# First product of a feed-forward network: seven products of quarters, or the plain product of 512 tokens at once

## The chip, the cores and the metric

The kernel runs on one core of a Trainium2 chip. The metric is the device time of one execution in microseconds; of several runs the median is given. The engines are named as the profile names them: PE (TensorE), PEld (its weight loads), DVE (VectorE), ACT (ScalarE), POOL (GpSimd), SP (SyncE, which issues most of the transfers).

## The reference

Two layers of a transformer work on 512 tokens of 1024 numbers and, in the first layer, on 256 context tokens beside them. A layer has a mixing half (a linear recurrence and differential attention) and a feed-forward half. Only the second concerns us here:

```python
def sq_relu_mlp(h, w1, w2):
    return jnp.square(jax.nn.relu(h @ w1)) @ w2      # w1: 1024 x 4096, w2: 4096 x 1024

f = sq_relu_mlp(modulate(rms_norm(x, g_pre_mlp[l]), sh2, s2), w_ff1[l], w_ff2[l])
x = x + g2 * rms_norm(f, g_post_mlp[l])
```

All is in float32. In layer 0 the context tokens take the same way, so that 768 tokens go through both products; in layer 1 only the 512 do.

## The kernel before

**Exact products.** Each float32 operand is split in a rounded upper part and the rest (`unit` for weights, lines 1496 and 1497: a copy on ScalarE, a subtraction on VectorE; `split_s` for the squares, lines 1653 and 1654). `mm3` (line 351) then adds three products for each pair: upper by upper, upper by rest, rest by upper.

**Blocks.** The 4096 hidden columns are taken in eight blocks `b` of 512. For a block, `ff1(b)` makes the squares `sq` (four tiles of 128 hidden columns by all tokens), and `ff2(b)` multiplies them with the second weights and adds to `acc` and `U2`. Block 0 has a plain first product (`ff1_plain`, in groups of 256 tokens), block 7 a plain second one (`end`, after `put`). So a layer runs `ff1_plain`, `ff2(0)`, `ff1(1)`, `ff2(1)`, up to `ff1(7)`, `end`.

**Seven products.** All other products go by the identities of Strassen and Winograd. Tokens, inner rows and columns are halved (`W` is half the tokens, 384 in layer 0 and 256 in layer 1), and seven products of quarters with sums of quarters replace the eight of the plain way. In `ff1` a product multiplies 512 rows by 256 columns of weights with half of the tokens: 24 matmuls of 128 x 128 weights with `W` columns. The sums cost extra work:

- sums of weights, on GpSimd, in `seven` (lines 1514 to 1518): four subtractions of 128 x 1024 for each block and each product, and seven units to split in place of four;
- sums of tokens, once a layer, between `ff2(0)` and `ff1(1)`: `tokens_sums` and `last_sum` (lines 1571 to 1600), on VectorE, GpSimd and ScalarE;
- sums of products: in `ff1` the `gather` of line 1621 on VectorE and a copy on ScalarE (line 1627), in `ff2` the `gather` of line 1687, and sums of squares on GpSimd (line 1669).

**Weights and places.** The weights come through six places of 1024 columns (`places`); `load` issues the transfer on SP's queue, `unit` splits. Split units lie in places of their own, used in turn (`wus`): three in layer 0, six in layer 1. `stream` hands out the units in the order of use, and `weights()` keeps three of them ahead. The products of `ff1` go to four banks of the accumulator memory (`pm`), those of `ff2` to four others (`pmg`); `bank` takes them in turn.

**Order.** The program is written in the order of the blocks; the framework reorders the instructions of the engines by its own model of time, within what the data allow, so that parts of `ff1(b + 1)` stand between those of `ff2(b)`.

Of the kernel before, what the change touches and what calls it, by code (L numbers as in the profile page):

```python
# [20 lines left out]
T = 768  # L21
TC = 256
EM = math.exp(-0.5)
# portions of projection work per portion of attention, by layer
FILLS = [2.3, 4.5]
# portions of adaLN work per recurrence step, by layer
# [28 lines left out]
def shape_consts():  # L55
# [8 lines left out]
    # the second direction's removal rows and columns lie reversed in each block of 32, so that its blocks, too,  # L64
    # are upper triangular
# [61 lines left out]
def ZI(a, p):  # L127
    """row of zd: a = 0, 1, 2 for r, k and the normalized k, p the pair of heads."""
    return (p // 2) * 6 + a * 2 + p % 2


class Fill:
    """Emits side work in small portions between the portions of the main work."""
# [31 lines left out]
class K:  # L165
# [91 lines left out]
    def ada_half(self, l, ch, hf, ps, tag):  # L257
        """512 adaLN columns for (c, c_ctx): columns 128*g.. as rows 32*g and 32*g+1, without bias."""
        nc = self.nc
        acc = ps.tile([128, 128], F32, name=self.n("adar"), tag=tag, bufs=1 if tag == "a" else 2)  # L260
        for kp in range(4):
            raw = self.raw(self.I["ada_w"][l, ch, hf, kp // 2][:, 2 * (kp % 2):2 * (kp % 2) + 2], [128, 2, 512])
            for k in range(2):
                for g in range(4):
                    nc.tensor.matmul(acc[32 * g:32 * g + 32, :], self.sc[:, 2 * kp + k, :],
                                     raw[:, k, g * 128:g * 128 + 128], start=(kp + k == 0), stop=(kp == 3 and k == 1),
                                     skip_group_check=True)
            if kp < 3:
                yield
        self.acc = acc  # L270
# [53 lines left out]
    def halves(self, src, shape):  # L324
        """loads of the two halves of a piece of weights."""
# [17 lines left out]
    def mm3(self, out, pairs, step=8, start=True):  # L343
        """out = sum over (sh, sl, mh, ml) of stationary^T moving, operands split exactly in two; added to what out
        holds if not `start`."""
# [15 lines left out]
    def new_hT(self):  # L361
        """split activations, one [128, T] view per 128 rows; the upper four lie first."""
# [7 lines left out]
    def norm(self, x, xn, junk):  # L370
        """xn = rms(x), the gain left out."""
# [7 lines left out]
    def norm_T(self, xn, group, mods, hT, pool, ps, toks):  # L379
        """two normed tiles [128,1024] of the tokens from toks on: modulated, transposed, split."""  # L380
# [22 lines left out]
    def layer(self, l):  # L403
        nc, I = self.nc, self.I
        last = l == L - 1
        if l == 0:
# [5 lines left out]
            with ExitStack() as es:  # L412
                # the first weights take the place of x
# [59 lines left out]
    def phase_wr(self, l, last):  # L473
# [33 lines left out]
        # The projections are cut into units: products into one bank, then its evacuation, which is emitted  # L507
        # only when the next unit's products have begun. Small units that follow from one wait in `posts`.
# [202 lines left out]
        def stream(order):  # L711
# [9 lines left out]
            for n, p in enumerate(order):  # L721
                wh, wl = w
                nxt = lambda: self.split_w(None, [128, 8, 256], feed(), wpw[(n + 1) % 2])
                if p >= 11:
                    both = order[n:n + 2] == [11, 12]
                    if both:
                        # the first tiles of both pieces run while the last tiles are still being normed
# [108 lines left out]
        def subln(j):  # L836
            """rms norm per head of a pair of heads, and its transposed store."""
# [88 lines left out]
    def recurrence(self, l, last, es, side):  # L926
        """opens the recurrence; its first sets go to `side`. Returns what emits the rest."""
# [4 lines left out]
        # a pool each: what comes after the recurrence may take a place as soon as it is free  # L932
# [13 lines left out]
        # zeros beside each head's rows and beside each half of the low-rank inputs let products run over 128 rows  # L946
# [15 lines left out]
        def prep_a(n, d, pp):  # L962
            """decay and rate of one pair of head pairs over one tile of 128 tokens, one direction."""
# [25 lines left out]
        def prep_b(n, d, pp, ld, th, ta):  # L989
            """chunk matrices of that pair from decay and rate."""  # L990
            need_y = not (last and n < 2)
            if pp == 0:
                # the same tile for every third group: each part is taken again as soon as it has been read
# [13 lines left out]
            # tokens in blocks of 32; the second direction's reversed in each  # L1007
# [16 lines left out]
            # half of it: the rate and its mix with k come doubled  # L1024
# [16 lines left out]
            # a bank for each head of the pairs: the heads lie in different rows  # L1041
# [37 lines left out]
        def relay(n, d):  # L1079
            # diagonal 32-blocks to one matrix per partition: (the block that the merge takes first, d, p, c, hf)  # L1080
# [12 lines left out]
        def eliminate(N, W, n):  # L1093
            """W, the rows 2i + (partition >= 64) of the strictly upper N, to those of (I - N)^-1."""
# [13 lines left out]
        def inv(n):  # L1108
            """inverses of the diagonal blocks of a group back into G, the transposed ones for the merge beside it."""
# [34 lines left out]
        def merge(n):  # L1144
# [11 lines left out]
            # the rows that each half of the partitions held come one after the other in TT  # L1156
# [87 lines left out]
        def finish(ti):  # L1244
# [8 lines left out]
            else:  # L1253
                # the sets of the groups that are over make room for it
# [49 lines left out]
        def rest():  # L1304
# [20 lines left out]
            for n in range(6):  # L1325
# [5 lines left out]
                for j in range(2):  # L1331
                    nst = 0
                    for _ in step(n, j):
# [5 lines left out]
                        # the next group but one: what it waits for is longer than a step  # L1339
# [19 lines left out]
    def post_norm(self, ob, Gb, x, junk):  # L1359
        """x += rms(ob) * Gb, in place in x."""  # L1360
# [15 lines left out]
    def phase_o(self, l, last):  # L1376
# [6 lines left out]
        with ExitStack() as es:  # L1383
# [18 lines left out]
            # what the first pairs need comes first  # L1402
# [39 lines left out]
    def phase_f(self, l, last):  # L1442
        """Most products go by Strassen's and Winograd's identities: seven products of halves of the tokens, of the rows
        and of the columns of a piece of weights give the eight that the product has. Tokens' sums s1 = a21 + a22,
        s2 = s1 - a11, s3 = a11 - a21, s4 = a12 - s2; weights' sums t1 = b12 - b11, t2 = b22 - t1, t3 = b22 - b12,
        t4 = b21 - t2; with u = a11 b11 + s2 t2 and v = u + s1 t1 the quarters are a11 b11 + a12 b21, u + s1 t1 + s4 b22,
        u + s3 t3 + a22 t4 and v + s3 t3."""
# [8 lines left out]
        # the halves of the tokens  # L1456
# [3 lines left out]
        with ExitStack() as es:  # L1460
            # the squares and their sums lie first: they end early, and the next layer's first weights take their place
# [16 lines left out]
            # six places of 1024 columns  # L1478
# [11 lines left out]
            def unit(src, m, pool=None):  # L1490
                """1024 columns of weights as m rows, split."""
# [8 lines left out]
            def seven(quarter, m, order, start=None):  # L1500
                """The weights of the seven products, in the order given."""
# [17 lines left out]
                # those that end first are taken again first  # L1519
                at = {"t1": 0, "t4": 1, "t3": 2, "b22": 3, "t2": 4}  # L1520
                places[:] = [places[i] for i in [5] + [at[k] for k in order if k in at]]

            def stream():
                for b in range(8):
                    if b:
                        yield from seven(lambda k, c: lines(k, c, b), 4, order1(b))
# [8 lines left out]

            def order1(b):
                return ["b11"] + (["t2", "b21"] if b > 1 else ["b21", "t2"]) + ["t1", "t3", "b22", "t4"]
# [33 lines left out]
            whole = lambda x, a, g, k: nc.vector.tensor_tensor(x, *(hT[f, g][:, k, H[a]].bitcast(F32) for f in "hl"), add)  # L1571

            def keep(x, S, k):
                nc.scalar.activation(S[0][:, k], x, AF.Copy)
                nc.vector.tensor_tensor(S[1][:, k], x, S[0][:, k].bitcast(F32), sub)

            def tokens_sums(S1, S2, pool):
                """The sums of the halves of the tokens, split; s3 takes a21's place."""
                S3 = tuple(hT[f, 0][:, :, H[1]] for f in "hl")
                f = nc.gpsimd.tensor_tensor  # L1580
                for k in range(4):
                    a11, a21, a22 = (pool.tile([128, W], F32, name=self.n("fx"), tag=f"x{i}") for i in range(3))
                    whole(a21, 1, 0, k)
                    whole(a22, 1, 1, k)
                    whole(a11, 0, 0, k)
                    f(a22, a21, a22, add)
                    f(a21, a11, a21, sub)
                    f(a11, a22, a11, sub)
                    keep(a22, S1, k)
                    keep(a11, S2, k)  # L1590
                    keep(a21, S3, k)
                return S3

            def last_sum(S2, S4):
                f = nc.gpsimd.tensor_tensor
                for k in range(4):
                    x = t2.tile([128, W], F32, name=self.n("fx"), tag="x", bufs=3 if last else 1)
                    whole(x, 0, 1, k)
                    for s in S2:
                        f(x, x, s[:, k].bitcast(F32), sub)  # L1600
                    keep(x, S4, k)

            def ff1(b, S):
                S1, S2, S3, S4 = S
                A = {(a, k): tuple(hT[f, k][:, :, H[a]] for f in "hl") for a in range(2) for k in range(2)}
                # u and v are in place in the quarters that come last
# [200 lines left out]
```

## Time and profile before

| | |
|---|---|
| median of 3 runs | 2538.57 us (2533.5 to 2541.35) |
| profiled execution | span 2535.5 us from its first instruction to its last; no time of its own is listed beside it |
| PE, DVE busy | 2264.5 us (89%), 1774.2 us (70%) |
| products of layer 0 from `ff2(0)` to `ff1(7)` | 876.3 to 1348.9 us |
| the same of layer 1 | 2123.2 to 2504.5 us |

The span is about 3 us shorter than the median of the runs. The window of a stage is cut at the first product with `fah` (the split squares) and at the end of `ff1(7)`.

### The profile page before, as it was taken

The page shows a single profiled execution, that of the slowest core. Times are in us where ns is not written, and L with a number is a line of the kernel's source. Part 1 is how long each engine was busy: PE and PEld are TensorE (multiplying, and loading weights), DVE is VectorE, ACT ScalarE, POOL GpSimd, SP SyncE. Part 2 cuts the span into 40 slices and gives each one's busy share as a digit, 9 for nine tenths or more (in the row PEclk, how much of TensorE's full clock was granted, in tenths as well). Part 3 has the DMA queues.
Part 4 walks back from the last instruction along what each step waited for, and adds up shares of the span by engine and source line. Part 5 has one row for each costly group of instructions (what it writes and reads, how often), then busy time and mean ns, then how long its engine had stood idle before and what let it go on. Part 6 is the DMA issues. An engine that isn't in the chain of part 4 may idle for free. (4 is left out here: it accounts for less than half of the span.)

```text
span 2535.5 us, 45036 instructions
## 1 busy us (share of the span) xinstructions
PE 2264.5 (89%) x17486; PEld 1948.9 (77%) x17486; DVE 1774.2 (70%) x2875; ACT 1246.6 (49%) x2551; POOL 1005.5 (40%) x1144
## 2 busy tenths in 40 slices
PE   6999998899889979999989999999799887798787
PEld 5897887777769868888878877788678776687676
DVE  5456459567655697777787465756665648999997
ACT  4345457544444444444435345655454445454543
POOL 1213225823122475555552322324621126665561
PEclk8999998788999999999999999997788798899999
DMA  6544344577685111111114353534676542112222
GB/s 263 150 132 110 124 132 108 129 186 190 170 240 185 51 59 67 67 67 67 67 58 171 108 162 101 156 108 109 165 191 146 151 167 84 67 67 100 91 76 108
DMA packets 291636, 313.75 MB, mean 124 GB/s; under 512 B 139680, under 2 KB 220896, under 8 KB 291424
## 3 DMA queue, kind: packets, MB, share of 16 engines
q1 hardware_dynamic: 280320, 284.66, 36.9%
q0 software_dynamic: 10240, 23.08, 4.8%
q8 instruction: 138, 2.26, 0.4%
q10 hardware_dynamic: 864, 3.15, 0.3%
q14 instruction: 74, 0.61, 0.1%
HBM read 257.04 MB, written 53.77 MB: 123 GB/s over the span
## 5 line engine op out<-in xcount | busy, mean ns | idle before, releaser
L1497 DVE TENSOR_TENSOR wl<-raw,wh 128x1024 fp32r<-128x1024 f32 x212 | 324.6, 1538 | 28.2 <-ACT wh L1496 28.1
L1496 ACT ACTIVATE wh<-raw 128x1024 fp32r<-128x1024 f32 x212 | 219.8, 1054 | 150.4 <-PE pf L351 45.2
L351 PE MATMUL pf<-wh,fah 128*128 128x512 f32 x570 | 238.4, 421 | 60.7 <-ACT fs L1546 18.4
L351 PE MATMUL pf<-wl,fah 128*128 128x512 f32 x570 | 235.5, 414 | 14.9 <-DVE wl L1497 14.8
L351 PE MATMUL pf<-wh,fal 128*128 128x512 f32 x570 | 224.5, 412 | 8.1 <-DVE fal L1654 8.1
L351 PE MATMUL pu<-hh,wh 128*128 128x512 f32 (+1 forms) x632 | 223.6, 354 | 3.4 <-DVE t L557 1.7
L351 PE MATMUL pu<-hh,wl 128*128 128x512 f32 (+1 forms) x632 | 218.1, 346 | 3.8 <-DVE wl L340 3.8
L351 PE MATMUL pu<-hl,wh 128*128 128x512 f32 (+1 forms) x632 | 217.8, 345 | 0.0
L351 PEld LDWEIGHTS pf<-wh,fah 128*128 128x128 f32 x570 | 113.6, 199 | 98.7 <-DVE acc L1687 22.2
L351 PE MATMUL pf<-hh,wh 128*128 128x256 f32 (+1 forms) x608 | 181.2, 307 | 8.6 <-ACT wh L1496 3.4
L351 PE MATMUL pf<-hh,wl 128*128 128x256 f32 (+1 forms) x608 | 180.5, 305 | 3.7 <-DVE wl L1497 3.4
L351 PE MATMUL pf<-hl,wh 128*128 128x256 f32 (+1 forms) x608 | 183.8, 305 | 0.0
L797 DVE TENSOR_REDUCE nm<-sc 128x1 f32<-128x768 f32 (+1 forms) x160 | 132.7, 842 | 70.3 <-PE sc L795 69.3
L799 ACT ACTIVATE e<-sc,nm 128x768 f32<-128x768 f32 (+1 forms) x160 | 131.1, 823 | 50.2 <-DVE nm L797 38.8
L321 POOL TENSOR_TENSOR rs<-ms,pw 128x1 f32<-128x1 f32 (+2 forms) x60 | 56.9, 951 | 233.4 <-DVE ms L319 232.2
L351 PEld LDWEIGHTS pf<-wl,fah 128*128 128x128 f32 x570 | 113.8, 200 | 40.3 <-DVE wl L1497 17.8
L680 POOL TENSOR_TENSOR zs<-zpad 128x512 f32<-128x512 f32 (+1 forms) x51 | 47.8, 937 | 240.2 <-ACT zpad L678 228.9
L351 PEld LDWEIGHTS pf<-wh,fal 128*128 128x128 f32 x570 | 112.5, 198 | 37.9 <-DVE fal L1654 12.3
L351 PEld LDWEIGHTS pu<-hh,wh 128*128 128x128 f32 x632 | 120.7, 191 | 21.5 <-DVE t L557 2.3
L351 PEld LDWEIGHTS pu<-hh,wl 128*128 128x128 f32 x632 | 120.8, 191 | 18.9 <-DVE wl L340 4.7
L832 PEld LDWEIGHTS po<-vn,pT 128*128 128x128 f32 x832 | 115.7, 209 | 23.6 <-ACT pT L818 13.7
L351 PEld LDWEIGHTS pu<-hl,wh 128*128 128x128 f32 x632 | 120.8, 191 | 14.3 <-issue 1.7
(281 smaller groups left out, 6658.4 us busy)
## 6 DMA issues: line engine op xcount, KB each, us to landing
raw<-in_w_ff SPq DMA_DIRECT2D x128, 512.0 KB
raw<-in_ada_w SPq DMA_DIRECT2D x96, 512.0 KB
raw<-in_w_in SPq DMA_DIRECT2D x52, 512.0 KB
ld<-zd SPq DMA_DIRECT2D x40, 384.0 KB
ks<-qd POOLq DMA_DIRECT2D x64, 192.0 KB, 5.7
zd<-zr SPq DMA_DIRECT2D x22, 384.0 KB
raw<-in_w_out SPq DMA_DIRECT2D x16, 512.0 KB
qs<-qd POOLq DMA_DIRECT2D x32, 192.0 KB, 6.0
```

What stands on the lines that cost most here:

```text
L321: nc.gpsimd.tensor_tensor(r, m, self.pw1.to_broadcast([128, cols]), ALU.pow)
L351: nc.tensor.matmul(out, a, b, start=(start and i == 0 and j == 0), stop=(i == n - 1 and j == 2), skip_group_check=not start)
L680: nc.gpsimd.tensor_tensor(s[:, sl], z[:, a - 1:b - 1], z[:, a + 1:b + 1], ALU.add)
L797: nc.vector.tensor_reduce(nm, sc, AX.X, ALU.max, negate=True)
L799: nc.scalar.activation(ee, sc, AF.Exp, bias=nm, accum_out=ls[:, br:br + 1])
L832: nc.tensor.matmul(po, pT[:, k * 128:k * 128 + 128], vn[:, k, h * 64:h * 64 + 64], start=(k == 0), stop=(k == nk - 1))
L1496: nc.scalar.activation(hi, src, AF.Copy)
L1497: nc.vector.tensor_tensor(lo, src, hi.bitcast(F32), sub)
```

## The change

In both layers the first product of blocks 1 to 7 is made plainly. `four` takes the place of `seven` for these weights: it loads and splits the four pieces of 1024 columns as they are. `ff1(b)` takes two units (the two halves of the 1024 rows, for 256 columns), and for each 128 of its columns adds 8 x 3 matmuls with 512 tokens at once, and, in layer 0, 8 x 3 more with the last 256. Each finished bank is squared by ScalarE (`square`: Relu, then Square in place). The sums of tokens and the tiles for them, the order of the seven products, and the sums of line 1621 go away. `ff2` and `end` stay. `ff1_plain` gets its extra place for weights in both layers, where before layer 1 had none.

```diff
+            def four(b):
+
+                ts = [load(2 * c + k, lines(k, c, b)) for c in range(2) for k in range(2)]
+                for t in ts:
+                    yield unit(t, 4)
+                places[:] = places[4:] + places[:4]
 
             def stream():
                 for b in range(8):
                     if b:
-                        yield from seven(lambda k, c: lines(k, c, b), 4, order1(b))
+                        yield from four(b)
                     if b < 7:
                         yield from seven(lambda k, c: cells(k, c, b), 2,
                                          ["b11", "b21", "t3", "t4", "t2", "t1", "b22"], None if b else self.normed)
...
-            def order1(b):
-                return ["b11"] + (["t2", "b21"] if b > 1 else ["b21", "t2"]) + ["t1", "t3", "b22", "t4"]
...
-            def tokens_sums(S1, S2, pool):
...
-            def last_sum(S2, S4):
...
-            def ff1(b, S):
-                S1, S2, S3, S4 = S
...
-                X = times(A[0, 0], weights())
-                for i in range(2):
-                    nc.scalar.copy(U[i], X[i])
-                for k in order1(b)[1:3]:
-                    if k == "t2":
-                        gather(U, times(S2, weights()), U)
-                    else:
-                        times(A[0, 1], weights(), X)
-                        for i in range(2):
-                            square(C11[i], X[i])
-                Y = times(S1, weights())
-                gather(V, Y, U)
-                X = times(S3, weights())
-                gather(V, X, V, True)
-                times(S4, weights(), Y)
-                gather(C12, Y, U, True)
-                times(A[1, 1], weights(), X)
-                gather(U, X, U, True)
+            def ff1(b):
+
+                for c in range(4):
+                    if c % 2 == 0:
+                        w = [weights(), weights()]
+                    cs = slice(c % 2 * 128, c % 2 * 128 + 128)
+                    for t0, t1 in ((i0 * 128, i0 * 128 + 512),) + (() if last else ((512, T),)):
+                        p = bank(t1 - t0)
+                        self.now(self.mm3(p, [(w[k // 4][0][:, k % 4, cs], w[k // 4][1][:, k % 4, cs],
+                                               hh[k][:, t0:t1], hl[k][:, t0:t1]) for k in range(8)]))
+                        square(sq[c][:, t0 - i0 * 128:t1 - i0 * 128], p)
...
             with ExitStack() as es2:
-                s_pool = lambda e: self.pool(e, "fh", 1)
-                s_tiles = lambda p: tuple(p.tile([128, 4, W], F32R, name=self.n("fh" + f), tag="f" + f) for f in "hl")
-                S2, S1 = [s_tiles(s_pool(es2)) for _ in range(2)]
-                # what comes before s4 lies in its place
-                with ExitStack() as es3:
-                    ff1_plain(None if last else self.pool(es3, "wx", 1))
+                ff1_plain(self.pool(es2, "wx", 1))
                 ff2(0)
-                with ExitStack() as e:
-                    for i in behind:
-                        e.enter_context(tc.issue_after(i))
-                    with ExitStack() as es3:
-                        S3 = tokens_sums(S1, S2, self.pool(es3, "fx", 3 if last else 2))
-                    S4 = s_tiles(s_pool(es2))
-                    last_sum(S2, S4)
-                S = S1, S2, S3, S4
                 for b in range(1, 8):
-                    ff1(b, S)
+                    ff1(b)
                     if b < 7:
                         ff2(b)
```

All other lines of the diff drop comments.

## Rows read from the trace of the kernel before

**Rows 1.** The page's table of engines: busy us, share of the span, instructions.

```profile
PE 2264.5 (89%) x17486; PEld 1948.9 (77%) x17486; DVE 1774.2 (70%) x2875; ACT 1246.6 (49%) x2551; POOL 1005.5 (40%) x1144
```

**Rows 2.** Windows: length, PE, PEld, DVE, ACT, POOL busy, granted clock, DMA share, GB/s.

```profile
1184.40:1247.87 63.47, 59.78 (x296) 52.44 (x295) 49.16 (x59) 29.60 (x46) 31.90 (x17) 1.00 0.20 67
2366.65:2417.39 50.74, 42.10 (x254) 36.56 (x253) 49.98 (x53) 25.39 (x47) 29.17 (x17) 0.97 0.26 83
876.30:1348.90 472.60, 431.22 (x2060) 377.27 (x2059) 386.96 (x445) 222.52 (x357) 250.46 (x130) 0.97 0.19 66
2123.20:2504.50 381.30, 314.41 (x1788) 271.95 (x1789) 368.71 (x401) 191.47 (x353) 223.54 (x131) 0.91 0.24 82
```

**Rows 3.** Timeline of ScalarE: the copies that mark a block; start, us.

```profile
1184.40 0.48 ACT L1627 COPY fs<-pf 128x384 f32<-128x384 f32 x1 [6.07 <-PE pf L351]
...
1247.87 0.48 ACT L1627 COPY fs<-pf 128x384 f32<-128x384 f32 x1 [6.08 <-PE pf L351]
...
2366.65 0.35 ACT L1627 COPY fs<-pf 128x256 f32<-128x256 f32 x1
...
2417.39 0.35 ACT L1627 COPY fs<-pf 128x256 f32<-128x256 f32 x1
```

**Rows 4.** Timeline of TensorE: first and last of runs without a gap.

```profile
1130.12 0.34 PE L351 MATMUL pf<-hh,wh 128*128 128x384 f32 x1
...
1150.26 0.34 PE L351 MATMUL pf<-hh,wl 128*128 128x384 f32 x1
...
1154.32 0.39 PE L351 MATMUL pf<-wh,fal 128*128 128x512 f32 x1
...
1173.14 0.40 PE L351 MATMUL pf<-wl,fah 128*128 128x512 f32 x1
...
1179.91 0.40 PE L351 MATMUL pf<-wh,fah 128*128 128x512 f32 x1
...
2235.20 0.28 PE L351 MATMUL pf<-hh,wh 128*128 128x256 f32 x1
...
2239.64 0.28 PE L351 MATMUL pf<-fhl,wh 128*128 128x256 f32 x1
```

**Rows 5.** Timeline of TensorE: two gaps, and a product after one.

```profile
1157.07 0.47 PE L351 MATMUL pf<-wh,fah 128*128 128x512 f32 x1 [2.36 <-DVE fu L1687]
...
1158.26 0.63 PE L351 MATMUL pf<-wl,fah 128*128 128x512 f32 x1
...
2406.72 0.47 PE L351 MATMUL pf<-wh,fah 128*128 128x512 f32 x1 [4.72 <-ACT fs L1546]
```

**Rows 6.** VectorE by line, one block of layer 1 (2366.65 to 2417.39).

```profile
L1497 DVE TENSOR_TENSOR wl<-raw,wh 128x1024 fp32r<-128x1024 f32 x14 | 22.8, 1642 | 0.8 <-ACT wh L1496 0.8
L1654 DVE TENSOR_TENSOR fal<-ts,fah 128x256 fp32r<-128x256 f32 x8 | 10.4, 1342 | 0.0
L1687 DVE TENSOR_TENSOR acc<-pf,acc 128x512 f32<-128x512 f32 x11 | 7.3, 675 | 0.0
...
L1621 DVE TENSOR_TENSOR fs<-pf,fs 128x256 f32<-128x256 f32 x10 | 4.0, 410 | 0.0
```

**Rows 7.** Instructions on the tiles fs and wl: ns min/median/max, first and last start.

```profile
L1621 DVE TENSOR_TENSOR fs<-pf,fs x140: 406/483/560, 942.5 to 2504.8; 128x384 f32<-128x384 f32 x70, 128x256 f32<-128x256 f32 x70
...
L1654 DVE TENSOR_TENSOR fal<-fs,fah x100: 405/620/2754, 869.4 to 2506.6; 128x384 fp32r<-128x384 f32 x50, 128x256 fp32r<-128x256 f32 x50
...
L1497 DVE TENSOR_TENSOR wl<-raw,wh x212: 1205/1224/3434, 799.4 to 2498.2; 128x1024 fp32r<-128x1024 f32 x106
```

**Rows 8.** GpSimd by line, the same block of layer 1.

```profile
L1514 POOL TENSOR_TENSOR raw<-raw,raw 128x1024 f32<-128x1024 f32 x3 | 7.2, 2409 | 5.7 <-DMA raw<-in_w_ff 5.7
```

**Rows 9.** VectorE by line, beginning of the stage in layer 1 (2118 to 2215).

```profile
L1575 DVE TENSOR_TENSOR fhl<-fx,fhh 128x256 fp32r<-128x256 f32 x12 | 15.0, 1276 | 0.5 <-ACT fhh L1574 0.5
L1571 DVE TENSOR_TENSOR fx<-hh,hl 128x256 f32<-128x256 f32 x16 | 11.8, 782 | 0.0
```

**Rows 10.** Timeline of TensorE, last block of layer 0.

```profile
1322.37 0.69 PE L351 MATMUL pf<-fhh,wl 128*128 128x384 f32 x1 [3.21 <-DVE wl L1497]
```

More of the change, by code (lines that the diff above doesn't have):

```diff
@@ L1569, in ff1_plain @@
                 places[:] = [places[i] for i in (1, 2, 3, 4, 5, 0)]
[L1571 to L1575, printed above, removed]
-            def tokens_sums(S1, S2, pool):
[L1579 to L1592, printed above, removed]
@@ L1594, in last_sum @@
-            def last_sum(S2, S4):
[L1595 to L1601, printed above, removed]
-            def ff1(b, S):
-                S1, S2, S3, S4 = S
-                A = {(a, k): tuple(hT[f, k][:, :, H[a]] for f in "hl") for a in range(2) for k in range(2)}
-                C11, C12, U, V = [[sq[2 * c + i][:, HS[a]] for i in range(2)] for a in range(2) for c in range(2)]
-                def times(a, w, old=None):
-                    res = []
-                    for i in range(2):
-                        cs = slice(i * 128, i * 128 + 128)
-                        p = old[i] if old else bank(W)
-                        self.now(self.mm3(p, [(w[0][:, k, cs], w[1][:, k, cs], a[0][:, k], a[1][:, k])
-                                              for k in range(4)], start=old is None))
-                        res.append(p)
-                    return res
-                def gather(d, p, x, done=False):
-                    for i in range(2):
-                        nc.vector.tensor_tensor(d[i], p[i], x[i], add)
-                        if done:
-                            square(d[i])
-                X = times(A[0, 0], weights())
-                for i in range(2):
-                    nc.scalar.copy(U[i], X[i])
-                for k in order1(b)[1:3]:
-                    if k == "t2":
-                        gather(U, times(S2, weights()), U)
-                    else:
-                        times(A[0, 1], weights(), X)
-                        for i in range(2):
-                            square(C11[i], X[i])
-                Y = times(S1, weights())
-                gather(V, Y, U)
-                X = times(S3, weights())
-                gather(V, X, V, True)
-                times(S4, weights(), Y)
-                gather(C12, Y, U, True)
-                times(A[1, 1], weights(), X)
-                gather(U, X, U, True)
```

## The prediction

> **What bounds the kernel now.** I read the engine table first [rows 1]: TensorE is busy 89% of the span, VectorE 70%. These are averages over very different stages, so the next view is busy time by stretch [rows 2], cut where the change acts: the feed-forward stage of each layer, from the first product with the second weights to the start of the last block's plain end. It lasts 472.6 us in layer 0 and 381.3 us in layer 1; each holds seven blocks (`ff2(0)` to `ff1(7)`). To cut one steady block I took the same copy (L1627, the evacuation that begins `ff1`) in two neighbouring blocks [rows 3]: 63.5 us in layer 0, 50.7 us in layer 1. In these windows [rows 2] the two layers differ. In layer 1 VectorE is busy 49.98 of 50.74 us: it is the bound there, and TensorE waits for it. In layer 0 VectorE has 14 us to spare, and TensorE is nearly always at work.
>
> Busy TensorE time contains modelled ends, so I price products from start to start in runs without a gap [rows 4]: 256 columns take (2239.64 - 2235.20) / 37 = 0.120 us, 384 take (1150.26 - 1130.12) / 116 = 0.174 us, and 512 take (1179.91 - 1173.14) / 29 = 0.233 us in a run beside other work. The 17 that follow the last of 384 columns up to 1154.32 need (1154.32 - 1150.26 - 0.174) / 17 = 0.229 us; I use 0.231. All at full clock.
>
> Products of one block, all three exact-split passes counted, before the change. Layer 0: `ff1` 7 x 2 x 4 x 3 = 168 of 384 columns = 29.2 us, `ff2` 7 x 3 x 2 x 3 = 126 of 512 = 29.1 us, sum 58.3. Layer 1: 168 of 256 = 20.2, 84 of 512 = 19.4, sum 39.6. So a steady block holds 5.2 us in layer 0 and 11.1 us in layer 1 that are no product. Where they lie [rows 5]: in layer 0 TensorE waits 2.36 us for VectorE in `ff2`, and then runs at the lower of its two clocks for a while (a product of 0.63 us where others take 0.40 [rows 4]); I put eight such at 8 x 0.23 = 1.8 us. In layer 1 the largest gap is 4.72 us at the start of `ff2`, after the last square of `ff1`.
>
> **What the change does to TensorE.** `ff1` becomes 4 x 8 x 3 = 96 products of 512 columns, and in layer 0 another 96 of 256. Layer 0: 96 x 0.231 + 96 x 0.120 = 33.7 us against 29.2, that is 4.5 more per block; the block's floor goes from 58.3 to 62.8. Layer 1: 22.2 against 20.2, 2.0 more; floor 41.6. Over seven blocks and two layers the plain products add 45 us to TensorE. This loss is certain; the rest must pay for it.
>
> **What it does to VectorE.** Per block it takes away three of fourteen weight splits (`wl`, L1497) and all ten sums of L1621. At today's means in layer 1 [rows 6] this is 3 x 1.64 + 4.0 = 8.9 us of 50.0, leaving 41.1. How far it can fall further is seen from the spread of single instructions [rows 7]: L1621, which reads one operand from PSUM, never exceeds 560 ns, while the splits, which read both from SBUF, go from 405 to 2754 ns (L1654) and from 1205 to 3434 (L1497). I put the long ones down to GpSimd, which reads SBUF at the same time. With no stretch VectorE would need 11 x 1.21 + 14 x 0.405 + 14 x 0.675 = 28.4 us. GpSimd loses half of its weight sums (four of eight of 2.4 us, [rows 8]), some 10 of its 29 us [rows 2], so I expect about 36. Either way VectorE ends below TensorE's 41.6 us, and TensorE becomes the bound in layer 1.
>
> **ScalarE** loses three weight copies per block; the evacuations become four wide Relu and four Square (eight of each in layer 0). It is busy 25 to 30 us per block [rows 2]: no bound. The loads stay four pieces per product, 67 and 83 GB/s in these windows; I cost them at nothing, hidden by the splits and products between. Were that cover gone, `raw` would be late for the copies of L1496, and the price would be a gap of the kind of the next paragraph.
>
> **What remains idle.** Layer 1's 4.72 us should go: today `ff2` waits for quarters finished by the last of the seven products; in the plain order the first product of `ff2` reads squares of the first two column tiles, done half an `ff1` earlier. The gap that stays is that of the bank whose partial sum must be read before more is added to it, with its slow clock. From 11.1 I keep 4.0 per block in layer 1 (bounds 1.5 and 6.0). In layer 0 I keep 3.0 of 5.2 (bounds 1.0 and 5.2), as part of the GpSimd work that delays VectorE there remains. So a block takes 65.8 us in layer 0 (was 63.5) and 45.6 in layer 1 (was 50.7).
>
> **The beginning.** Before `ff1(1)` the sums of halves of the tokens are made (L1571 to L1600). Seven steady blocks would be 7 x 63.5 = 444.4 and 7 x 50.74 = 355.2 us; the stages take 472.6 and 381.3, so their beginnings (and, in layer 0, a late stall) cost 28.2 and 26.1 us. In layer 1 the token sums keep VectorE for 11.8 + 15.0 us [rows 9] and a little more while it is saturated. The change drops them. The first block still has its first weights to split and no lead; I leave 8 us in layer 0 (bounds 4 and 14) and 9 in layer 1 (5 and 14).
>
> **Sum.** Layer 0: 7 x 65.8 + 8 = 468.6 us, 4.0 less than 472.6. Layer 1: 7 x 45.6 + 9 = 328.2, 53.1 less than 381.3. Together 57 us off a span of 2535.5; the median of the runs shown, 2538.57, lies 3.1 above that span, so 2538.6 - 57 = 2481.5, and I say 2481. With all lower bounds: layer 0 7 x 63.8 + 4 = 450.6 (-22), layer 1 7 x 43.1 + 5 = 306.7 (-75): 2442. With all upper: 7 x 68.0 + 14 = 490 (+17), 7 x 47.6 + 14 = 347 (-34): 2522.
>
> **Rivals.** *VectorE stays the bound in layer 1.* If the 12 GpSimd instructions left per block (four of 2.4 us and eight sums of tokens' squares, some 9 us) each hold VectorE for their whole length, it needs 28.4 + 18.7 = 47.1 us, and at today's 98.5% share a block takes 47.8: 7 x 47.8 + 9 = 343.6, the gain shrinks to 4 + 38 = 42 us, 2497. For it: the stretched splits above. Against: at today's means VectorE needs 41 only. The Trainium skill states this as a rule (SBUF — State Buffer, section "Who interferes with whom"): a VectorE instruction with two SBUF inputs and a GpSimd one that reads SBUF exclude each other for a whole instruction, whoever comes second waits. This case's spread agrees (2754 against at most 560 ns); by the strictest reading this rival is the forecast, and I give it 13%.
>
> *Three places for split weights in layer 0.* Plain `ff1` holds two units at once and needs the fourth when the first has just come free, 12 products of 256 columns (1.4 us) before the next pair begins; its copy and split must fit into that and 12 of 512 (2.8 us). With stretched splits they don't: a stall like the 3.21 us on `wl` late in layer 0 [rows 10] and 1.8 us of slow clock in each block, 7 x 5.0 = 35 us; the gain falls to 22 us, 2516. Against: an unstretched copy and split take under 2.5 us. 7%.
>
> *The turn from `ff1` to `ff2` stalls (slower).* The last tile's Relu, Square and split lie in one chain on ScalarE and VectorE; if `ff2` must wait for it as today in layer 1 (4.72 us [rows 5] and 1.8 of slow clock), each of 14 blocks pays 6.5 us, 91 in all, against a gain of 57: 34 slower, 2572. It decides from 57 / 14 = 4.1 us per block on. Against it: one product of `ff2` (12 or 18 matmuls, 2.8 or 4.2 us) needs none of the last tile and covers most of that chain. 6%; that it costs about 4 us a block, and nothing is left, 4%.
>
> *Nearly no idle time remains* (lower bounds): 2442 or a little below, 6%.
>
> **Chances.** Forecast 64%, VectorE 13, weight places 7, turn 6 and 4, lower bounds 6. Measurement tells about 0.3% (7.6 us) from no change. Faster: 64 + 13 + 7 + 6 = 90%; same 4%; slower 6%. The range 2444 to 2520 takes in the forecast's bounds, the VectorE and the weight-place rival, and leaves out the turn and half of the lower bounds.
>
> **What would show it.** Right: no L1571 to L1621 lines; `pf<-hh,wh` of 512 columns started 0.23 us apart; steady blocks of 64 to 68 us in layer 0, longer than before, and 43 to 48 in layer 1, shorter; VectorE under 90% there; splits with a lower mean; `ff2(0)` to `ff1(1)` without saturated VectorE. Wrong: 512-column products further apart than 0.24 us or at the lower clock, TensorE idle before `fah` or before the second pair of weights in each block, a VectorE still at 98% in layer 1, or a beginning as long as before (waiting for first weights or their GpSimd sums, not for the token sums).

## The result and the profile after

| | median, us | range of the runs, us | runs |
|---|---|---|---|
| before, on the same chip | 2539.2 | 2533.5 to 2541.35 | 4 |
| after | 2450.86 | 2442.96 to 2465.64 | 4 |

The ratio is 0.9648, 95% interval 0.9612 to 0.9685: 88 us off, where 57 were forecast. The time lies inside the range (2444 to 2520), near its fast end.

The profiled execution after has a span of 2463.9 us and is the slowest of the four. The page's table of engines, to be held against [rows 1]:

```profile
PE 2273.2 (92%) x17150; PEld 1919.2 (78%) x17150; DVE 1516.6 (62%) x2629; ACT 1173.8 (48%) x2393; POOL 806.8 (33%) x1048
```

TensorE is busy longer than before (2273.2 against 2264.5) in a shorter span. VectorE lost 258 us and GpSimd 199. Busy time by stretch of the kernel after (length, PE, PEld, DVE, ACT, POOL busy, granted clock, DMA share, GB/s). The first two stretches are four blocks of layer 1 and three of layer 0; the other two are the stages of layer 0 and layer 1, cut as in [rows 2]:

```profile
2221.27:2386.64 165.37, 165.37 (x722) 135.15 (x721) 129.40 (x156) 84.98 (x133) 74.39 (x48) 1.00 0.31 102
1066.83:1259.81 192.98, 189.36 (x956) 158.91 (x955) 112.47 (x138) 75.81 (x124) 64.49 (x37) 1.00 0.20 66
879.90:1333.85 453.95, 443.85 (x2229) 371.38 (x2227) 267.67 (x325) 187.62 (x308) 146.25 (x82) 1.00 0.21 68
2129.90:2427.00 297.10, 293.17 (x1261) 238.34 (x1261) 230.28 (x279) 155.92 (x248) 122.77 (x81) 0.99 0.33 108
```

The blocks were cut at the same evacuation in neighbouring blocks, now a Relu; timeline of ScalarE, kernel after (start, length):

```profile
1066.83 0.60 ACT L1549 ACTIVATE fs<-pf 128x512 f32<-128x512 f32 x1 [5.18 <-PE pf L351]
...
1131.08 0.60 ACT L1549 ACTIVATE fs<-pf 128x512 f32<-128x512 f32 x1 [5.23 <-PE pf L351]
...
2221.27 0.58 ACT L1549 ACTIVATE fs<-pf 128x512 f32<-128x512 f32 x1
...
2262.45 0.58 ACT L1549 ACTIVATE fs<-pf 128x512 f32<-128x512 f32 x1
...
2386.64 0.58 ACT L1549 ACTIVATE fs<-pf 128x512 f32<-128x512 f32 x1
```

A block of layer 0 takes 192.98 / 3 = 64.33 us (before 63.47), one of layer 1 165.37 / 4 = 41.34 (before 50.74). In layer 1 TensorE has no idle time left in four blocks; VectorE is busy 129.40 / 4 = 32.4 us of 41.3, where it was 49.98 of 50.74 [rows 2]. GpSimd fell from 29.17 to 18.6 us per block. The bound has moved from VectorE to TensorE, and 180 products of 512 columns in 41.34 us make 0.2297 us each.

The stages, cut from the first product with the second weights to the last of `ff1(7)`'s `pf<-hl,wh`, in the two profiled executions:

| us | before | after | difference |
|---|---|---|---|
| stage of layer 0 | 472.2 | 453.7 | -18.5 |
| between the stages | 774.7 | 796.3 | +21.6 |
| stage of layer 1 | 381.1 | 296.7 | -84.4 |
| end of layer 1's stage to the last instruction | 31.2 | 37.3 | +6.1 |

With 3.6 more ahead of layer 0's stage this is the span's -71.6. The last line of the table is a shift: 24 products of the final block that used to stand between the last ones of `ff1(7)` now come behind them. The 21.6 us between the stages lie in work that the change does not touch, and are taken up at the end.

### The profile page after: what moved, and what is told of

It is laid out like the page before. It is cut to its first block, busy times and chain, and to the rows that moved or that the text cites. A ratio compares the mean times of both kernels' runs of the same rounds, so it can differ in the third digit from the quotient of the medians.

```text
span 2463.9 us, 43744 instructions
## 1 busy us (share of the span) xinstructions
PE 2273.2 (92%) x17150; PEld 1919.2 (78%) x17150; DVE 1516.6 (62%) x2629; ACT 1173.8 (48%) x2393; POOL 806.8 (33%) x1048
## 4 chain that ended last, share of the span: by engine, by line
PE 68%; DMA 10%; DVE 9%; ACT 4%; issue 3%; SPq 2%; POOL 2%; POOLq 0%; DVEq 0%; ACTq 0%
PE pf L351 31%; PE pu L351 15%; PE po L351 4%; DMA raw<-in_ada_w 2%; PE pb L1046 2%; PE po L832 2%; DMA TT<-dt 2%; PE X L1186 1%; PE pb L977 1%; PE adar L265 1%; PE sc L795 1%; DVE wl L1497 1%; PE X L1226 1%; DVE nm L797 1%; PE X L1189 1%
## 5 line engine op out<-in xcount | busy, mean ns | idle before, releaser
L1497 DVE TENSOR_TENSOR wl<-raw,wh 128x1024 fp32r<-128x1024 f32 x170 | 255.8, 1507 | 125.6 <-ACT wh L1496 124.8
L351 PE MATMUL pf<-hl,wh 128*128 128x512 f32 (+1 forms) x832 | 282.1, 342 | 0.0
L351 PE MATMUL pf<-hh,wh 128*128 128x512 f32 (+1 forms) x832 | 280.5, 342 | 0.5 <-ACT hh L397 0.5
L351 PE MATMUL pf<-hh,wl 128*128 128x512 f32 (+1 forms) x832 | 275.7, 342 | 0.0
L1496 ACT ACTIVATE wh<-raw 128x1024 fp32r<-128x1024 f32 x170 | 179.2, 1058 | 162.0 <-PE pf L351 143.9
L351 PE MATMUL pf<-wh,fah 128*128 128x512 f32 x570 | 225.3, 398 | 11.5 <-DVE fu L1630 7.2
L351 PEld LDWEIGHTS pf<-hl,wh 128*128 128x128 f32 x832 | 156.6, 188 | 20.0 <-DVE hl L399 0.2
L351 PEld LDWEIGHTS pf<-hh,wl 128*128 128x128 f32 x832 | 156.0, 188 | 20.0
L351 PEld LDWEIGHTS pf<-hh,wh 128*128 128x128 f32 x832 | 155.3, 188 | 20.4 <-ACT hh L397 0.8
L799 ACT ACTIVATE e<-sc,nm 128x768 f32<-128x768 f32 (+1 forms) x160 | 130.7, 821 | 53.7 <-DVE nm L797 44.3
L1630 DVE TENSOR_TENSOR acc<-pf,acc 128x512 f32<-128x512 f32 x155 | 104.2, 682 | 53.9 <-PE pf L351 53.3
```

Of the source, the lines that this page charges most:

```text
L351: nc.tensor.matmul(out, a, b, start=(start and i == 0 and j == 0), stop=(i == n - 1 and j == 2), skip_group_check=not start)
L799: nc.scalar.activation(ee, sc, AF.Exp, bias=nm, accum_out=ls[:, br:br + 1])
L1496: nc.scalar.activation(hi, src, AF.Copy)
L1497: nc.vector.tensor_tensor(lo, src, hi.bitcast(F32), sub)
L1630: nc.vector.tensor_tensor(d, p, d, add)
```

## The experiments

Stages and steady blocks of all kernels, read as above (us):

| kernel | span | stage, layer 0 | between | stage, layer 1 | block, layer 0 | block, layer 1 |
|---|---|---|---|---|---|---|
| before | 2535.5 | 472.2 | 774.7 | 381.1 | 63.5 | 50.7 |
| after | 2463.9 | 453.7 | 796.3 | 296.7 | 64.3 | 41.3 |
| plain in layer 1 alone | 2441.7 | 473.7 | 771.0 | 295.9 | | |
| plain in layer 0 alone | 2524.5 | 453.7 | 774.3 | 379.2 | | |
| before, no weight sums | 2484.9 | 457.9 | 775.7 | 340.2 | 63.5 | 44.5 |
| before, no token sums | 2506.8 | 452.8 | 779.4 | 360.5 | 63.5 | 51.1 |
| after, GpSimd's work back, tied | 2457.3 | 453.8 | 779.3 | 312.6 | 64.3 | 42.6 |
| after, VectorE's work back, tied | 2488.1 | 453.7 | 788.7 | 328.9 | 64.3 | 46.3 |
| after, 256 tokens at once | 2467.0 | 457.6 | 793.0 | 303.2 | | 42.3 |
| after, three places in layer 1 | 2481.0 | 453.7 | 796.9 | 317.6 | | 44.3 |
| after, six places in layer 0 | 2441.2 | 446.7 | 788.5 | 296.6 | 62.4 | |

**One layer at a time.** The kernel before, with the new `four` and the new `ff1` in one layer only:

```diff
-                        yield from seven(lambda k, c: lines(k, c, b), 4, order1(b))
+                        yield from four(b) if last else seven(lambda k, c: lines(k, c, b), 4, order1(b))
```

> Layer 1 plain, layer 0 as before. Theory (each layer's stage stands for itself: in layer 1 VectorE was the bound, now TensorE): layer 1's stage from ff2(0) to the end of ff1(7) takes 297 us as in the changed kernel (381 before), layer 0's 472 as before; total 84 us less than before, some 2455. Rival (part of the gain is given back in layer 1's recurrence because layer 0 ends earlier): the stretch between the two stages takes 774 us as before, not 796 as in the profile of the changed kernel. If that stretch is again 20 us longer, or shorter, it varies from run to run and has nothing to do with layer 0.

> Layer 0 plain, layer 1 as before. Theory: layer 0's stage takes 454 us (472.6 before), steady blocks of 64.3 us (63.5 before), all of the gain from the beginning without token sums; layer 1's stage 381. Total 19 us less than before, some 2520. Rival (the gain of layer 0 comes back in the recurrence behind it): total within 8 us of before, the stretch between the stages 20 us longer than 774.

Layer 1 alone: 2453.77 us (2443.74 to 2460.21), ratio 0.9674, interval 0.9627 to 0.972. Layer 0 alone (`if not last`): 2523.84 (2513.16 to 2533.94), ratio 0.9938, interval 0.9913 to 0.9964. Each stage is what it is in the full change, and the other is within 2 us of before. Five sixths of the gain are layer 1's. Layer 0 is also a small gain (0.6%), though its blocks are longer: the stage's beginning pays for it. The stretch between the stages stays near 774 us in both profiles: neither layer's change by itself is seen to lengthen it.

**The arithmetic that the seven products cost, taken out of the kernel before.** First GpSimd's sums of weights for `ff1`, then the sums of tokens at the beginning of the stage; the products, splits and evacuations stay.

```diff
-                t2 = place(4)
+                t2 = place(4) if sums else b22
...
                     yield unit(t[k], m)
+                    if not sums:
+                        continue
...
-                S = S1, S2, S3, S4
+                S = [tuple(hT[f, k][:, :, H[a]] for f in "hl") for a, k in ((1, 0), (0, 0), (1, 0), (0, 1))]
```

> The kernel before without GpSimd's sums of the first product's weights: the seven units are split as they were loaded (so the result is not the product), the order of the products, the token sums and VectorE's instructions stay. Theory (VectorE stretched by GpSimd): VectorE falls from 50 to about 44 us per block of layer 1, block 50.7 to 45 to 47; layer 0's block 63.5 to 61 to 62. Rival (late quarters): the gap of 4.7 us at the start of ff2 stays, block of layer 1 above 48.

One run: 2486.72 beside 2537.95 for the kernel before. Windows of three blocks of layer 1 and three of layer 0 (columns as above), kernel before without weight sums:

```profile
2240.78:2374.40 133.62, 120.24 (x742) 104.60 (x741) 120.18 (x153) 73.58 (x137) 58.81 (x36) 1.00 0.30 95
1055.78:1246.28 190.50, 180.57 (x884) 158.72 (x883) 147.66 (x178) 88.79 (x140) 63.82 (x36) 0.99 0.20 67
```

VectorE by line in the first of these windows:

```profile
L1497 DVE TENSOR_TENSOR wl<-raw,wh 128x1024 fp32r<-128x1024 f32 x41 | 57.4, 1408 | 4.6 <-ACT wh L1496 4.6
...
L1656 DVE TENSOR_TENSOR fal<-ts,fah 128x256 fp32r<-128x256 f32 x22 | 12.3, 587 | 0.0
```

In layer 1 GpSimd's busy time falls from 29.17 to 58.81 / 3 = 19.6 us per block, and VectorE's, whose own instructions are unchanged, from 49.98 to 120.18 / 3 = 40.1: GpSimd's 9.6 us cost VectorE 9.9. Both VectorE and the block fell further than expected. The split of `ts` (sums of squares) went from 1342 ns [rows 6] to 587. Two thirds of the block's gain are here (50.7 to 44.5, of 41.3 in all) while VectorE still has all its splits and sums. What TensorE still waits for in this window (us in total, times, longest):

```profile
PE pf L351 <- DVE fs L1623: 5.9, 4, 2.0
PE pf L351 <- ACT fs L1547: 4.8, 3, 1.6
PE pf L351 <- DVE fal L1656: 1.6, 3, 0.5
PE pf L351 <- DVE wl L1497: 1.1, 3, 0.4
```

No wait is longer than 2.0 us: the gap of 4.72 us at the start of `ff2` [rows 5] is gone although the order of the seven products is unchanged, so the rival of this run falls. What is left lies for the most part at the sums of the seven products in `ff1` (`fs`, 5.9 of 13.4 us) and at ScalarE's work on `fs`. For layer 0 the expectation failed: the block stays at 63.5, and TensorE keeps its gap at `fu` (the sums of products in `ff2`). That gap is then not owed to the weight sums of `ff1`.

> The kernel before without the sums of halves of the tokens (L1571 to L1600): its seven products multiply halves themselves, so the result is not the product; all else is done. Theory (the long beginnings are the token sums on VectorE): the beginnings shrink from 28 and 26 us to 5 to 10 each, the steady blocks stay at 63.5 and 50.7 us, total 35 to 45 us less than before. Rival (the beginning waits for first weights and their GpSimd sums): less than 15 us in all.

2502.25 us (2497.69 to 2508.85), ratio 0.9858, interval 0.9817 to 0.9899: 38 us less, as expected. The stages shrink by 19.4 and 20.6 us at unchanged blocks (a window of two in layer 1: VectorE 97.42 of 102.14 us). So the beginning is worth about 20 us in each layer, as the prediction had it (28.2 to 8 and 26.1 to 9).

**The removed work put back into the kernel after.** Three kernels put back per `ff1` GpSimd's four sums of 1024 columns (a), VectorE's 13 instructions (b), or both (c), on tiles of their own:

```diff
-                for t in ts:
+                for n, t in enumerate(ts):
                     yield unit(t, 4)
+                    for _ in range((3, 1, 0, 0)[n]):
+                        nc.gpsimd.tensor_tensor(dum[0], dum[1], dum[2], sub)
```

> The changed kernel with four GpSimd subtractions of 128x1024 put back into each block's first product, on tiles that nobody else reads. It tells what GpSimd's work costs VectorE. Theory (VectorE's means were stretched by GpSimd): in layer 1 VectorE's busy time rises from 32.7 to 36 to 39 us per block, the block stays at 41.3 to 42.5 since TensorE is the bound. Rival (gaps came from the order of the seven products and their late quarters): VectorE rises as well, block 41.3. A block of 44 or more would say that the stretch alone makes the gaps.

> The changed kernel with VectorE's removed work put back on tiles that nobody else reads: three subtractions of 128x1024 and ten of 128 by half of the tokens in each block's first product, all with both operands in SBUF. Theory (VectorE's amount of work was the bound): VectorE rises from 32.7 to about 42 us per block in layer 1, the block to 43 to 46. Rival (order of the seven products): block 41.3 to 42, since nobody waits for this work.

> The changed kernel with both put back, GpSimd's four and VectorE's thirteen instructions per first product. Theory (VectorE with GpSimd's stretch was the bound in layer 1, whatever the order): VectorE 46 to 50 us per block, block 47 to 51, so nearly all of layer 1's steady gain is gone although the products are plain; layer 0's block 65 to 68. Rival (order of the products): block in layer 1 under 44.

One run each: 2510.53, 2528.03 and 2618.73 us. None answers the question. The tile `dum` in the stretch from 2100 to 2300 us of (a) (count, ns min/median/max, first and last start):

```profile
L1529 POOL TENSOR_TENSOR dum<-dum,dum x28: 2340/2558/3449, 2127.3 to 2284.0; 128x1024 f32<-128x1024 f32 x28
```

All 28 instructions of seven blocks ran at the front of a stage that lasted from 2140.9 to 2471.9: waiting for no data, they were placed ahead in a bunch. The stages of the three kernels grew by 16 to 76 us, and in (a) the blocks behind the bunch took 41.3 as without it. So the work was put back once more, now on the weights themselves right behind their use, in two kernels, GpSimd's part in one and VectorE's in the other (`ts` are the four raw tiles, `f` GpSimd's subtraction; W is 256 in layer 1, 384 in layer 0):

```diff
                     yield unit(t, 4)
+                    if n == 0:
+                        f(ts[0], ts[2], ts[0], sub)
+                        f(dum, ts[3], ts[0], sub)
+                        f(dum, ts[3], ts[2], sub)
+                    elif n == 1:
+                        f(ts[1], ts[1], dum, sub)
...
+                    for m in [1024] * (n < 3) + [W] * (3, 3, 2, 2)[n]:
+                        nc.vector.tensor_tensor(t[:, :m], t[:, :m], t[:, :m], add)
```

> As the third run, but each of GpSimd's four subtractions now reads and overwrites weights of its own block that have been split (the product doesn't need them any more), so that it can't run ahead in a bunch. Theory (TensorE is the bound, GpSimd only stretches VectorE): in layer 1 VectorE rises from 32.7 to 36 to 40 us per block, the block stays at 41.3 to 43; layer 0's block 64.3 to 66. Rival (the stretch alone makes VectorE late): block of layer 1 at 45 or more.

> As the fourth run, but VectorE's thirteen extra instructions work in place on weights of their own block that have been split. Theory (what counts in layer 1 is the sum of VectorE's work against TensorE's 41.3 us): VectorE at 41 to 43 us, block 43 to 46. Rival (order and late quarters, not the amount): block under 42.

One run each, 2459.09 and 2489.9 us beside 2534.99 for the kernel before. Three blocks of layer 1 with GpSimd's work back, windows and then VectorE by line (2266 to 2390):

```profile
2247.85:2375.74 127.89, 124.88 (x542) 101.19 (x541) 113.87 (x118) 62.36 (x101) 89.88 (x48) 1.00 0.30 99
```

```profile
L1497 DVE TENSOR_TENSOR wl<-raw,wh 128x1024 fp32r<-128x1024 f32 x33 | 55.4, 1685 | 13.7 <-ACT wh L1496 13.7
L1604 DVE TENSOR_TENSOR fal<-ts,fah 128x256 fp32r<-128x256 f32 x24 | 22.6, 956 | 0.0
```

The same lines of the kernel after, same stretch:

```profile
L1497 DVE TENSOR_TENSOR wl<-raw,wh 128x1024 fp32r<-128x1024 f32 x33 | 52.6, 1595 | 7.7 <-ACT wh L1496 7.7
...
L1597 DVE TENSOR_TENSOR fal<-ts,fah 128x256 fp32r<-128x256 f32 x25 | 11.5, 476 | 0.0
```

Four blocks of layer 1 with VectorE's work back, windows and then waits in them (us in total, times, longest), one of ScalarE and two of TensorE:

```profile
2266.77:2451.91 185.14, 169.93 (x707) 136.39 (x708) 161.08 (x216) 83.95 (x132) 76.42 (x42) 0.96 0.26 89
```

```profile
ACT wh L1496 <- DMA raw<-in_w_ff: 10.3, 5, 3.1
...
PE pf L351 <- DVE wl L1497: 8.0, 4, 4.3
...
PE pf L351 <- DVE fu L1632: 7.1, 2, 3.5
```

GpSimd's work back (18.6 to 30.0 us per block) lengthens VectorE's by 5.6 us, the `ts` split from 476 to 956 ns, and the block by only 1.3: with TensorE the bound, most of the stretch is hidden. VectorE's work back (32.4 to 40.3) costs 5.0 us per block: TensorE then waits for split weights and for the gather again, though VectorE is busy only 87% of the block (VectorE stayed a little under what was expected, the block came out a little over). The 5.0 us are not VectorE's amount of work alone: the work in place also holds the weight tiles longer, and ScalarE's copies wait 10.3 us for transfers in this window, where in the four blocks of the kernel after they wait for none.

An alternative was that the plain order of `ff1`, and not the smaller load, removed the gaps. The order is the plain one in this kernel, and gaps are back, so order alone does not remove them. With about the same VectorE time per block TensorE idles about as much in either order: 4.5 us at 40.1 us of VectorE with the seven products (the kernel before without weight sums), 3.8 at 40.3 here. That the order has no part is not shown: the sums of the seven products, at which 5.9 us of waits lay there, are gone with it, and no run has the seven products at the small load of the kernel after.

**Half the columns per product.**

```diff
-                    for t0, t1 in ((i0 * 128, i0 * 128 + 512),) + (() if last else ((512, T),)):
+                    for t0, t1 in ((t, t + 256) for t in range(i0 * 128, T, 256)):
```

> The changed kernel with 256 tokens at once in all plain products, so 192 matmuls of 256 columns per block of layer 1 in place of 96 of 512, and 288 in layer 0. By the spacings 0.120 and 0.230 us: 1.0 us more per block in layer 1 (42.3) and 1.0 in layer 0, 7 us more in each stage. A rival by which twice as many weight loads bound the narrow ones would give 0.19 us each: blocks of 56 and 84 us.

One run: 2468.84 us. The window of three blocks of layer 1:

```profile
2262.43:2389.21 126.78, 126.78 (x830) 115.89 (x829) 92.84 (x117) 67.91 (x124) 56.97 (x36) 1.00 0.33 100
```

A block takes 42.26 us, 0.9 more, TensorE again without idle time. So the width as such is worth about 1 us a block in layer 1; the rest of the gain does not come from it. Layer 0's stage is 3.9 us longer, where 7 were expected.

**Places for split weights.** Layer 1 of the kernel after has six, layer 0 three. Three in layer 1, then six in layer 0:

```diff
-            wus = self.wus + [self.pool(es, "wu", 1) for _ in range(4 if last else 1)]
+            wus = self.wus + [self.pool(es, "wu", 1) for _ in range(1)]
...
                 ff1_plain(self.pool(es2, "wx", 1))
+                more = [] if last else [self.pool(es2, "wu", 1) for _ in range(3)]
+                wus.extend(more)
                 ff2(0)
...
+            wus[:] = [p for p in wus if p not in more]
```

> The changed kernel with three places for split weights in layer 1 as well, in place of six. The rival of the prediction (plain products hold two units at once, so three places stall each block for some 3 us and a slow clock) would give 45 to 47 us per block; theory (a copy and a split fit into the products in between) 41.3 to 43.

One run: 2482.78 us. Three blocks of layer 1, windows and then the waits of TensorE:

```profile
2251.49:2384.50 133.01, 128.41 (x542) 100.66 (x541) 102.49 (x117) 63.12 (x100) 58.38 (x36) 1.00 0.30 95
```

```profile
PE pf L351 <- DVE acc L1630: 4.5, 9, 0.8
```

A block takes 44.3 us, 3.0 more, between what the two theories gave; the small waits are on sums that VectorE reads late. Why three places make them late is not shown.

> The changed kernel with six places for split weights in layer 0 in place of three, in the room that the token sums left. Theory (the gap of 1.2 us per block of layer 0 that is left comes of GpSimd's last weight sum, which stands at the turn to ff2 because its split had to wait for a place): the sum runs earlier, blocks of layer 0 fall from 64.3 to about 63.0, stage 454 to 445, total 9 us less than the changed kernel. Rival (the gap is VectorE's own queue at the turn): 64.3 as now. A third: the deeper place changes nothing since only three units are emitted ahead.

2442.42 us (2431.58 to 2451.11), ratio 0.962, interval 0.9584 to 0.9655. Three blocks of layer 0, windows:

```profile
1050.54:1237.77 187.23, 187.23 (x956) 159.21 (x955) 105.31 (x138) 76.18 (x123) 65.05 (x37) 1.00 0.21 68
```

A block takes 62.4 us, 1.9 less than after, and TensorE is never idle. What the places moved is seen in the timelines. Kernel after, where TensorE waits in each block of layer 0 (TensorE, then VectorE, then GpSimd):

```profile
1082.07 0.47 PE L351 MATMUL pf<-wh,fah 128*128 128x512 f32 x1 [1.16 <-DVE fu L1630]
...
1077.90 3.42 DVE L1497 TENSOR_TENSOR wl<-raw,wh 128x1024 fp32r<-128x1024 f32 x1
1081.24 1.87 DVE L1630 TENSOR_TENSOR fu<-pf,fu 128x512 f32<-128x512 f32 x3
...
1077.64 2.60 POOL L1518 TENSOR_TENSOR raw<-raw,raw 128x1024 f32<-128x1024 f32 x1 [5.86 <-issue]
1080.20 1.99 POOL L1612 TENSOR_TENSOR ts<-fs,fs 128x384 f32<-128x384 f32 x1
```

With six places, the same part of a block (VectorE, then GpSimd):

```profile
1071.05 1.22 DVE L1497 TENSOR_TENSOR wl<-raw,wh 128x1024 fp32r<-128x1024 f32 x1
1072.18 1.28 DVE L1630 TENSOR_TENSOR fu<-pf,fu 128x512 f32<-128x512 f32 x2
...
1048.33 2.39 POOL L1518 TENSOR_TENSOR raw<-raw,raw 128x1024 f32<-128x1024 f32 x1
```

After: while GpSimd makes the last sum of `ff2`'s weights, the split beside it takes 3.42 us, the gather of `fu` is late, and TensorE waits 1.16. With six places that sum is over 20 us earlier, the split takes 1.22, and the wait is gone. This is the fastest kernel of the study; its interval overlaps that of the change, and it is the stage of layer 0 (453.7 to 446.7) that shows the difference.

## Why the prediction was right, and which term was off

**Direction and mechanism: right.** Layer 1's bound moved from VectorE to TensorE; layer 0's blocks grew (63.5 to 64.3); the beginnings shrank; products of 512 columns go 0.23 us apart. Timeline of TensorE, kernel after, first and last of a run of 30 intervals in the last `ff1` (7.00 / 30 = 0.233 us):

```profile
2419.81 0.40 PE L351 MATMUL pf<-hh,wh 128*128 128x512 f32 x1
...
2426.81 0.40 PE L351 MATMUL pf<-hh,wl 128*128 128x512 f32 x1
```

**The floors: right.** Forecast 41.6 and 62.8 us; measured where TensorE is never idle, 41.3 in layer 1 (after) and 62.4 in layer 0 (six places).

**The step that was mis-sized: "What remains idle".** It kept 4.0 us per block in layer 1 and 3.0 in layer 0. Measured: none, and 64.3 - 62.4 = 1.9. In layer 1 that is below even the lower bound of 1.5. The two stages gave 103 us where 57 were forecast; of the 46 between, this term makes 7 x (45.6 - 41.3) = 30 in layer 1 and 7 x (65.8 - 64.3) = 10 in layer 0, and the beginnings the other 6. I carried over gaps at sums that VectorE has to read, as if they belonged to TensorE's program. They were VectorE being late. The reason that I gave for the loss of the 4.72 us, the order of the products, was not needed: the kernel before without weight sums lost that gap in its steady blocks, in the old order. TensorE's idle time per block of layer 1 (a window's length less PE's busy time) goes with VectorE's load, if not by its share alone:

| layer 1, per block | VectorE's share | TensorE idle, us |
|---|---|---|
| before | 98% | 8.6 |
| before, no weight sums | 90% | 4.5 |
| after, GpSimd's work back | 89% | 1.0 |
| after, VectorE's work back | 87% | 3.8 |
| after | 78% | 0 |

The forecast's own VectorE (about 36 of 45.6 us, 79%) was close to the measured share, but a share alone would not have told me that the gap goes: in layer 0 VectorE is busy 77% of a block before (49.16 of 63.47 us [rows 2]) and 58% after, and TensorE waits for it in both.

**VectorE: a little high.** 32.4 us measured, about 36 forecast, 28.4 the least. The stretch by GpSimd is shown from both sides: 9.6 us of GpSimd's work cost VectorE 9.9 in the kernel before, and 11.4 cost 5.6 in the kernel after. The rule that the prediction took from the Trainium skill (SBUF — State Buffer, section "Who interferes with whom") agrees with the first pair, where VectorE was nearly always at work. In the second VectorE has pauses, and only half of GpSimd's time shows up.

**The beginnings.** Taken as stage less seven blocks, 453.7 - 7 x 64.33 = 3.4 and 296.7 - 7 x 41.34 = 7.3 us; 8 and 9 were forecast, and the first lies just under its lower bound of 4. The prediction's reason, the token sums, is confirmed by the kernel without them.

**The rivals.** *VectorE stays the bound* is refuted (78%). *The turn stalls* is refuted: no gap there in layer 1, and the one gap of layer 0's block lies at the gather. *Places for split weights* was partly true, in another place and at a smaller price: not 5.0 us ahead of the second pair of weights but 1.9 us per block, through a GpSimd sum that comes late. *Nearly no idle time remains* is what happened in layer 1, and the time was on its way there.

**What ran against the gain.** The stages and the shifted products say 18.5 + 84.4 - 6.1 = 97 us for the pair of profiles; the medians say 88. That the time came out inside the range is partly luck: the stages alone gave 103 us, more than the 97 of all lower bounds together, and 2539.2 - 103 = 2436 would have been below 2444. What the two profiles show against the gain, the products shifted behind the stage and the longer stretch between the stages, was not in the prediction. The medians of the two kernels with one plain layer lie 86.7 and 16.6 us below theirs, 103 together, but their intervals do not separate that from 88.

The stretch between the stages took 774.7 us before and 796.3 after, and from 771 to 804 over all kernels. The same part of the recurrence in two profiles, before and then after (windows, columns as above):

```profile
1748.90:1798.90 50.00, 44.21 (x363) 35.71 (x364) 24.86 (x48) 22.79 (x61) 38.21 (x96) 0.73 0.65 181
1798.90:1848.90 50.00, 36.71 (x613) 30.13 (x609) 37.79 (x101) 25.20 (x61) 31.06 (x82) 0.80 0.64 150
```

```profile
1733.80:1783.80 50.00, 46.39 (x266) 36.88 (x266) 25.20 (x44) 23.13 (x60) 35.34 (x80) 0.61 0.58 156
1783.80:1833.80 50.00, 38.53 (x522) 31.10 (x521) 28.45 (x78) 16.40 (x39) 27.73 (x78) 0.64 0.61 135
```

TensorE was granted 0.61 and 0.64 of its clock after, 0.73 and 0.80 before, and got through fewer products in each 50 us. The clock of these windows does not settle the length, though: the kernel before without weight sums was granted 0.62 and 0.69 there, and its stretch took 775.7. Kernels whose layer 0 has the seven products lie at 771 to 779, those with a plain layer 0 at 774 to 804. Whether some of it is tied to the change stays open; no run separates this from the scatter.

## What to carry to other kernels

Before cutting products by sums, price the sums on every engine they touch: here, in layer 1, GpSimd's help cost the saturated VectorE as many microseconds as GpSimd worked (9.9 for 9.6 per block), more than the 2.0 that TensorE saved. When a change moves the bound from one engine to another, go through the old gaps by their releaser: those that end on the relieved engine can go with its load and should not be carried over as they are. Here all went in layer 1; in layer 0 one stayed, at a VectorE split beside a late GpSimd sum. Work added for an experiment must be tied to data of its place, or it runs ahead in a bunch and measures something else.

## What was not expected of the hardware

- Split into products of 256 columns, with twice as many weight loads, a block of layer 1 needed only 0.9 us more (42.26 against 41.34): about 0.120 us per product against 0.2297 for 512 columns.
- One VectorE split of 128x256 with both operands in SBUF took 1342 ns on average in the kernel before and 476 after, with GpSimd busy 29.2 and 18.6 us per block: with a third of GpSimd's time gone it was shorter by almost two thirds. With GpSimd's work put back (30.0 us per block) it took 956.
- An untouched stretch of sparse products took 771 to 804 us from kernel to kernel; in the two profiles compared above its granted clock was 0.61 to 0.64 where it took 796.3, and 0.73 to 0.80 where it took 774.7, but 0.62 to 0.69 in another kernel where it took 775.7.
